# Three small tiles are padded, so that feature tiles and weight tiles start at the same place within 64 bytes

## The chip, the core and the metric

The kernel runs on one core of a Trainium2 chip. The metric is the device time of one execution in microseconds (us). Engines are named as in the profile: PE is TensorE (PEld its weight loads), DVE is VectorE, ACT is ScalarE, POOL is GpSimd, SP issues the DMAs. SBUF is the on-chip memory of 128 partitions; a tile occupies the same bytes of each partition, and "place" below means the byte in a partition at which a tile starts.

## The reference, cut to what matters

Two transformer blocks run after each other on 512 grid tokens (and 256 context tokens in the first) of 1024 features: feed-forward, a parallel mixer of two recurrences, another feed-forward; then a state-space mixer beside sparse attention, and a mixture of experts. All of it is made of dense products such as

```python
def swiglu(h, w1, w2):
    g, u = jnp.split(h @ w1, 2, axis=-1)
    return (jax.nn.silu(g) * u) @ w2

proj = h_all @ w_in
lat_out = merged[:, n_ctx:] @ w_out
```

in float32.

## The kernel before, in words

Features lie transposed, with the features on the partitions and the tokens along the free axis. To multiply in float32 quality, each operand is split in two numbers of the faster type float32r: hi (the rounded value) and lo (the rest). A product is then three matmuls into one PSUM bank, and this helper issues nearly all of them:

```python
def mm3(self, out, wh, wl, xh, xl, start, stop):
    nc.tensor.matmul(out, wh, xh, start=start, stop=False)
    nc.tensor.matmul(out, wh, xl, start=False, stop=False)
    nc.tensor.matmul(out, wl, xh, start=False, stop=stop)
```

The three are lines 210, 211 and 212 of the profile. Weights are the stationary operand (128 x 128, which is 512 bytes per partition), the features the moving one (256 or 512 columns, 1024 or 2048 bytes). In rows of the profile `pppa<-lath,whi` reads: into PSUM bank pppa, moving tile lath, stationary tile whi. Weights come by DMA into `wraw`; `wsplit` (lines 191 and 192) makes `whi` on ACT and `wlo` on DVE. Feature tiles are `lath`/`latl` (grid tokens, normed) and `ctxh`/`ctxl` (context tokens), `hh`/`hl` (hidden features of a feed-forward), `y0h`/`y0l` and `y1h`/`y1l` (the two halves of the state-space output), `mh`/`mlo` (the merged branches). Two places swap the roles: `proj_tok` (lines 552 to 554) streams the weights past stationary features, and the experts' gather (2084, 2085) streams a one-hot `oh` past `n2h`/`n2l`. The experts' own products (2109, 2132) are plain float32 and run two by two on half of the array's columns.

The stages, in us from the span's start: modulation, norms and the first feed-forward 0 to 640 (768 tokens: products of 512 and of 256 columns), the first mixer 640 to 1200, the second feed-forward 1200 to 1560 (512 tokens), norms and the start of the second block 1560 to 1690, state-space and attention 1690 to 2400, the output projections 2400 to 2520, routing 2520 to 2590, experts to the end. A scheduler sets the order of the instructions on each engine; that order is the same in both programs.

What differs is where tiles lie. Pools on the left of SBUF (constants, features) are laid one after the other from the constants on, and a tile takes a whole number of 32 bytes. Pools on the right (`wraw`, `whi`, `wlo`, temporaries) are counted from the top and don't move. Three tiles decide whether what comes after them starts at 0 or at 32 within 64 bytes: `eps` (the norms' epsilon, in the constants, ahead of everything on the left), `inv` (rotary frequencies, ahead of the second feed-forward's hidden tiles) and `frs` (the last norm's scale, ahead of `y1h`, the experts' weights `ew`, `oh`).

The starts of the main operands in the two programs, in bytes, with the place within 64 and within 256 bytes:

```
tile                          before   in 64  in 256   after    in 64  in 256
whi (first of its buffers)    186336   32     224      186336   32     224
lath                          21504    0      0        21536    32     32
ctxh                          54272    0      0        54304    32     32
hh of the first feed-forward  125120   0      192      125152   32     224
hh of the second              123104   32     224      123168   32     32
y0h                           58368    0      0        58400    32     32
y1h                           123360   32     224      123424   32     32
mh                            21504    0      0        21536    32     32
oh (moving)                   197088   32     224      197152   32     32
n2h (stationary)              74752    0      0        74784    32     32
yhl (moving)                  91136    0      0        91168    32     32
ohT (stationary)              207456   32     96       207520   32     160
ew (moving, plain float32)    123360   32     224      123424   32     32
xg (stationary)               58368    0      0        58400    32     32
hT (stationary)               a place of 32 within 64 in both
```

Buffers of one name lie a multiple of 256 bytes apart, and so do the blocks that a matmul takes out of them, so that one row speaks for all.

The program's float32r matmuls of 512 and 256 columns, and the experts' plain ones, by the places of moving and stationary operand within 64 bytes (a few odd ones left out):

```
columns   moving, stationary   before -> after      matmuls in the program
512       0, 32                -> 32, 32            5488 (lath, hh of the first feed-forward, y0, mh, yhl)
512       32, 32               -> 32, 32             648 (hh of the second feed-forward, y1)
256       0, 32                -> 32, 32            2664 (ctx, lath, mh, hh of the first feed-forward)
256       32, 0                -> 32, 32            1280 (proj_tok, the experts' gather)
256       32, 32               -> 32, 32             144 (hh of the second feed-forward, at its end)
512 plain 32, 0                -> 32, 32             256 (ew, xg)
512 plain 32, 32               -> 32, 32             128 (ew, hT)
```

By stage, the matmuls of the first sort are 1464 in the first feed-forward, 626 in the first mixer, 982 in the second feed-forward, 262 up to 1690 us, 1529 in state-space and attention, 303 in the output projections, the rest later.

Of the kernel before, what the change touches and what calls it, by code (L numbers as in the profile page):

```python
# [10 lines left out]
F32 = mybir.dt.float32  # L11
# [19 lines left out]
L = 512  # L31
# [9 lines left out]
class Kern:  # L41
# [6 lines left out]
    def banks(self, stage):  # L48
        """the eight banks of PSUM, by use, from here on"""
        pa, pb, pf = PS[stage]  # L50
        assert pa + pb + pf == 8
        if PS[max(stage - 1, 0)] == PS[stage] and stage:
            return
        self.psx.close()
        self.ps = self.psx.enter_context(self.tc.tile_pool(name="ps", bufs=1, space=PSUM, reuse_waits="tile"))
        self.psb = {"pa": pa, "pb": pb, "pf": pf}
# [13 lines left out]
    @contextmanager  # L70
    def later(self, n):
        """what is issued here yields to the next n instructions"""
        p = self.tc.cur_priority
        self.tc.cur_priority = p + n
        yield
        self.tc.cur_priority -= n
# [13 lines left out]
    def tmpf(self, name="tmpf"):  # L90
        """for work that fills gaps: not in line with the rest"""
# [10 lines left out]
    def setup(self):  # L102
# [7 lines left out]
        self.eps = cst.tile([128, 1], F32, name="eps")  # L110
        nc.vector.memset(self.eps, 1e-6)
# [8 lines left out]
    def lower_bounds(self, l0, l1, vec):  # L120
        """softmax over two rows of logits, first entry (columns [128, 8])"""
# [12 lines left out]
        # log(1 - lb)  # L134
# [4 lines left out]
    def columns(self, name, items, tag="pa"):  # L139
        """items: (key, ap of n*128 contiguous values, n); gives columns [128, n] of each."""  # L140
# [4 lines left out]
        r = 0  # L145
# [14 lines left out]
    def to_T(self, dst, src, ntok):  # L160
        """src DRAM [ntok,1024] -> dst [128, 8, ntok]"""
# [36 lines left out]
    def cols(self, w, c0, n):  # L198
        """columns c0..c0+n of w [K, N] as [128, K/128, n]"""
# [3 lines left out]
    def wrows(self, w, r0, nb):  # L203
        """row blocks r0.. (128 each) of w [K, N] as [128, nb, N]"""
# [9 lines left out]
    mvp = None      # pool of the rows' own room  # L214
# [4 lines left out]
    def silu_cols(self, aps, name):  # L219
        """columns of silu(c): [128, 8, len(aps)]"""  # L220
# [30 lines left out]
    def matvec(self, dst, w, sc, n, c0, nb, bias, tag=None):  # L251
        """dst [128, nb, n] = columns c0.. (nb blocks of 128) of silu(c) @ w + bias (bias [128, nb])"""
# [31 lines left out]
    def sumsq(self, x, n, tag, w2=None):  # L284
        """sums over the features of x^2 and, if asked for, of w2 x^2 [128 (all rows the same), n] in PSUM; x [128, 8, n]"""
# [20 lines left out]
    def table(self, name):  # L306
        """the activation table that comes next, after what has been issued"""
# [12 lines left out]
    def rstd(self, p, n, dim, name="rstd", dst=None, both=False, then=None):  # L320
        """1/sqrt(p/dim + eps) from PSUM p [128, n]; both: with the table that has both functions; then: the next table"""
# [7 lines left out]
    def halves(self, x, A, B):  # L329
        """the parts of norm_split for the grid's tokens, by half"""  # L330
        return [(x[:, :, t:t + 256], 256, A, B, t) for t in (0, 256)]

    def stats(self, parts):
        """1/rms of each of parts [(x, n, ..)]"""
# [4 lines left out]
    def norm_split(self, batches, hi, lo, rs=None):  # L339
        """batches: [[(x, n, A, B, t0)]]: hi + lo[:, :, t0:t0 + n] = x * rstd * A + B"""  # L340
# [21 lines left out]
    def ffn(self, w1, w2, hi, lo, segs, ends, begin=None, fill=()):  # L362
        """segs: [(t0, n, x, gate)]: x += gate * swiglu(hi + lo); gate already holds the half.
        ends: the segments for the first and last products, smaller for what waits and comes next"""
# [113 lines left out]
FB = (1, 1, 2)     # matrix-vector products beside a head of the mLSTM, of the HGRN, beside its last head  # L478
# [8 lines left out]
class Mix1:  # L487
    """HGRN2 and mLSTM over the context (256 tokens) and the grid (512 tokens)."""

    def mix1(self, i, hi, lo, vec, mrg, early):  # L490
        """hi, lo: [128, 8, 768] (grid tokens 0..511, context 512..767); mrg: DRAM [8, 128, 512]"""
# [36 lines left out]
    # one 128-column block, feature-major: fn(psum [128, n], t0, n)  # L528
# [11 lines left out]
    # token-major, 256 columns: fn(psum [128, 256], chunk)  # L540
# [16 lines left out]
    def wtok(self, w, c0):  # L557
        """256 columns of w, as two halves over k"""
# [10 lines left out]
    # ---------------------------------------------------------------- mLSTM  # L569
    def ml_project(self, i, w, vec):  # L570
# [10 lines left out]
        # q (chunks 0, 1: grid only) and k (chunks 2, 3), padded for the convolutions  # L581
# [3 lines left out]
        for ch in (2, 3, 0, 1):  # L585
# [15 lines left out]
            if ch == 3:  # L601
                # by half of the grid: the second one's norm comes later
# [8 lines left out]
        # v, token-major, with a column of ones  # L611
# [40 lines left out]
    def ml_scan(self, i, w, vec):  # L652
        nc, ml = self.nc, self.ml
        R = 56                                   # rows (dir, chunk, head): 0..23 forward, 32..55 backward
        # token-major gates, then rows
# [17 lines left out]
        # log sigmoid(f) = min(f, 0) - log1p(exp(-|f|))  # L673
# [8 lines left out]
        # cumulative sums and maxima within the chunks  # L682
# [6 lines left out]
        # the maximum carried from chunk to chunk  # L689
# [7 lines left out]
        ch = ml.tile([1, 4, 64], F32, name="ch")     # sum, maximum, carried m, carry weight  # L697
# [14 lines left out]
        mm = ml.tile([128, 2], F32, name="mmc")[:R]  # carried m, last maximum  # L712
# [5 lines left out]
        cwp = ml.tile([128, 2, 16], F32, name="cwp")  # [dir, (chunk, pair)]  # L718
# [17 lines left out]
        # states  # L736
# [13 lines left out]
        for c in (4, 5, 0, 1, 2, 3):  # L750
# [13 lines left out]
            if c == 5:  # L764
                # context states -> first grid chunk of each direction
# [17 lines left out]
        # queries scaled for the states  # L783
# [11 lines left out]
        # scores, outputs  # L795
# [70 lines left out]
    # ---------------------------------------------------------------- HGRN2  # L866
# [8 lines left out]
    def hg_front(self, i, w, vec, h):  # L875
        """the projections of a head and what follows from them alone"""
# [12 lines left out]
        # of each direction: the sums of the log decays, B, and A = B + log k (backward) or B - log k (forward)  # L889
# [3 lines left out]
        for d in range(2):  # L893
# [32 lines left out]
            # the keys themselves, both directions added  # L926
# [9 lines left out]
    def hg_back(self, vec, h, mrg, front):  # L936
# [3 lines left out]
        # pairs at every level  # L940
# [6 lines left out]
        for d in range(2):  # L947
            B, A, Tt = BA[:, 1 + d, :L], BA[:, 3 * d, :L], Ta[:, d, :8]
            X, Y = BA[:, 2 * d, :L], BA[:, 2 * d + 1, :L]   # what the first and the second halves take
            sq, sk = (1, 0) if d == 0 else (0, 1)      # which half holds the queries / the keys  # L950
# [46 lines left out]
            # states between the chunks  # L997
# [3 lines left out]
            # U: from the chunk's start, V: to its end; queries and keys or keys and queries  # L1001
# [20 lines left out]
            # context  # L1022
# [15 lines left out]
            # transposed keys  # L1038
# [24 lines left out]
        # scores of both directions in one [key, query] tile  # L1063
# [19 lines left out]
        # norm over the head, gate  # L1083
# [11 lines left out]
        else:  # L1095
            # nothing reads the grid's rows any more
# [22 lines left out]
class Mix2:  # L1119
    LAT = [(0, 512)]  # L1120

    # ------------------------------------------------------------- rope tables
    def rope_tables(self, i, pool, cosd, sind):
        """cos and sin of the positions' angles, [128, 512], to DRAM"""
        nc = self.nc
        inv = pool.tile([128, 1], F32, name="inv")
# [24 lines left out]
        # sin(r) = sign(r) sin(min(|r|, pi - |r|)), cos(r) = sin(pi/2 - |r|)  # L1151
# [14 lines left out]
    # ------------------------------------------------------------- projections  # L1166
    def proj_col(self, w, c0, n, fn, tag="pa"):
        """n columns from c0, feature-major over the 512 tokens: fn(psum [n, 512])"""
# [8 lines left out]
    def proj_halves(self, w, items):  # L1177
        """proj_col of up to three items (c0, n), first for one half of the tokens, then for the other: their PSUMs"""
# [1363 lines left out]
```

## Time and profile before

| what | value |
|---|---|
| runs of the kernel before | 2944.2, 2953.55, 2950.13 us; median 2950.13 |
| span of the profiled execution (first to last instruction) | 2933.2 us; no other time of that execution is on record |
| PE busy | 2799.7 us, 95% of the span |
| PE weight loads | 2114.3 us, 72%, beside the matmuls |
| DVE, ACT, POOL busy | 53%, 34%, 9% |
| DMA | 373.95 MB, mean 127 GB/s |

Busy time of PE counts overlapped matmuls once; the pace of a run of matmuls is read from their starts in the timeline, since the end of one lies behind the start of the next.

### The profile page before, as it was taken

How to read it: one execution, taken by the hardware profiler on the slowest of the kernel's cores; microseconds unless marked ns; L12 is line 12 of the kernel's file. 1: busy time of each engine (PE TensorE's matmuls, PEld its weight loads, DVE VectorE, ACT ScalarE, POOL GpSimd, SP SyncE). 2: the span in 40 equal slices, each digit the busy share in tenths (PEclk: the TensorE clock that was granted, in tenths of full speed). 3: DMA queues.
4: the chain of work that ended last, by engine and by line, in shares of the span. 5: the costliest groups of instructions: out<-in, count | busy, mean ns of one | idle time of the engine just before them, and what ended most of it. 6: DMA issues, size and time to landing. Idle time of an engine off the chain costs nothing. (4 is left out here: it accounts for less than half of the span.)

```text
span 2933.2 us, 41489 instructions
## 1 busy us (share of the span) xinstructions
PE 2799.7 (95%) x16545; PEld 2114.3 (72%) x16546; DVE 1548.8 (53%) x3002; ACT 1000.1 (34%) x1793; POOL 257.3 (9%) x301
## 2 busy tenths in 40 slices
PE   7999999999998889999998999999999999989997
PEld 5788888889786666688887777666777768855553
DVE  6333333357358995543436556655666654543334
ACT  5211112144236663322224334444444533311112
POOL 2000000002001211000001000111222120000000
PEclk9999999999999899999999999999999999999999
DMA  7422122142512348533334332101233466378885
GB/s 259 139 87 79 51 65 65 59 129 72 151 52 65 85 155 284 170 94 98 95 90 142 95 92 74 30 12 45 80 101 104 131 204 203 110 272 280 289 305 186
DMA packets 386997, 373.95 MB, mean 127 GB/s; under 512 B 20321, under 2 KB 316645, under 8 KB 386546
## 3 DMA queue, kind: packets, MB, share of 16 engines
q1 hardware_dynamic: 386802, 371.28, 40.3%
q8 instruction: 131, 2.15, 0.3%
q14 instruction: 64, 0.52, 0.1%
HBM read 343.70 MB, written 27.53 MB: 127 GB/s over the span
## 5 line engine op out<-in xcount | busy, mean ns | idle before, releaser
L191 ACT CAST whi<-wraw 128x1024 fp32r<-128x1024 f32 x277 | 285.8, 1042 | 758.9 <-PE pppa L211 340.0
L210 PE MATMUL pppa<-lath,whi 128*128 128x512 f32 (+4 forms) x1344 | 521.9, 389 | 15.0 <-ACT whi L191 6.0
L211 PE MATMUL pppa<-latl,whi 128*128 128x512 f32 (+3 forms) x1344 | 519.9, 387 | 4.7 <-DVE latl L358 3.5
L212 PE MATMUL pppa<-lath,wlo 128*128 128x512 f32 (+3 forms) x1344 | 515.2, 385 | 0.5 <-DVE wlo L192 0.5
L192 DVE TENSOR_TENSOR wlo<-wraw,whi 128x1024 fp32r<-128x1024 f32 (+1 forms) x273 | 330.8, 1218 | 255.0 <-ACT whi L191 245.5
L210 PEld LDWEIGHTS pppa<-lath,whi 128*128 128x128 f32 (+3 forms) x1344 | 252.5, 188 | 81.1 <-ACT whi L191 12.9
L211 PEld LDWEIGHTS pppa<-latl,whi 128*128 128x128 f32 (+2 forms) x1344 | 252.2, 188 | 67.6 <-DVE latl L358 5.0
L212 PEld LDWEIGHTS pppa<-lath,wlo 128*128 128x128 f32 (+2 forms) x1344 | 252.1, 188 | 58.3 <-issue 4.5
L211 PE MATMUL pppb<-hl,whi 128*128 128x512 f32 (+1 forms) x576 | 195.4, 341 | 0.0
L210 PE MATMUL pppb<-hh,whi 128*128 128x512 f32 (+1 forms) x576 | 193.1, 344 | 0.0
L212 PE MATMUL pppb<-hh,wlo 128*128 128x512 f32 (+1 forms) x576 | 191.6, 341 | 0.0
L416 DVE SCALAR_TENSOR_TENSOR xT<-pppb,sG,xT 128x512 f32<-128x512 f32 (+1 forms) x144 | 96.8, 690 | 135.0 <-PE pppb L212 134.8
L396 DVE TENSOR_TENSOR hf<-sg,pppa 128x256 f32<-128x256 f32 (+1 forms) x68 | 39.7, 584 | 232.5 <-PE pppa L212 232.0
L210 PE MATMUL pppf<-lath,whi 128*128 128x512 f32 x320 | 129.7, 405 | 7.9 <-ACT lath L1823 2.9
L2109 PE MATMUL pppa<-ew,xg 128*64 128x512 f32 x512 | 131.2, 597 | 0.0
L210 PE MATMUL pppa<-ctxh,whi 128*128 128x256 f32 (+1 forms) x440 | 124.1, 282 | 5.4 <-DVE W L912 5.1
L212 PE MATMUL pppf<-lath,wlo 128*128 128x512 f32 x320 | 127.8, 400 | 0.6 <-DVE wlo L192 0.6
L211 PE MATMUL pppf<-latl,whi 128*128 128x512 f32 x320 | 128.0, 400 | 0.0
L210 PEld LDWEIGHTS pppb<-hh,whi 128*128 128x128 f32 x576 | 108.0, 188 | 27.3 <-issue 5.8
L212 PE MATMUL pppa<-ctxh,wlo 128*128 128x256 f32 (+1 forms) x440 | 124.2, 282 | 0.0
L211 PE MATMUL pppa<-ctxl,whi 128*128 128x256 f32 (+1 forms) x440 | 123.8, 281 | 0.3 <-POOL ctxl L356 0.3
L211 PEld LDWEIGHTS pppb<-hl,whi 128*128 128x128 f32 x576 | 108.4, 188 | 16.1 <-issue 3.4
(698 smaller groups left out, 5195.5 us busy)
## 6 DMA issues: line engine op xcount, KB each, us to landing
wraw<-in_ffn_w_dram SPq DMA_DIRECT2D x132, 512.0 KB, 4.0
wraw<-in_w_in_dram SPq DMA_DIRECT2D x102, 512.0 KB, 4.2
ew<-in_w_exp_gate_dram SPq DMA_DIRECT2D x64, 512.0 KB, 9.6
ew<-in_w_exp_up_dram SPq DMA_DIRECT2D x64, 512.0 KB, 8.7
ew<-in_w_exp_down_dram SPq DMA_DIRECT2D x32, 1024.0 KB, 11.2
mraw<-in_w_mod_dram SPq DMA_DIRECT2D x40, 512.0 KB, 7.0
wraw<-in_w_mod_dram SPq DMA_DIRECT2D x32, 512.0 KB, 4.3
mraw<-in_w_ada_dram SPq DMA_DIRECT2D x32, 512.0 KB, 7.0
```

The source lines that it names most:

```text
L191: nc.scalar.copy(hi[:, :n], raw[:, :n])
L192: (nc.gpsimd if pool else nc.vector).tensor_sub(lo[:, :n], raw[:, :n], hi[:, :n].bitcast(F32))
L210: nc.tensor.matmul(out, wh, xh, start=start, stop=False)
L211: nc.tensor.matmul(out, wh, xl, start=False, stop=False)
L212: nc.tensor.matmul(out, wl, xh, start=False, stop=stop)
L396: nc.vector.tensor_mul(h[:, :n], sg[:, :n], pp[1])
L416: nc.vector.scalar_tensor_tensor(x[:, o, :], p[:, :n], gate[:, o:o + 1], x[:, o, :], op0=OP.mult, op1=OP.add)
L2109: nc.tensor.matmul(ph[x * 64:x * 64 + 64, :], xg[:, k, pr * 128 + x * 64:pr * 128 + x * 64 + 64], wts[k // 4 * 2 + x][:, k % 4, :], start= ...
```

## The change

Three tiles get 16 columns of float32 (64 bytes) where they had one or four (4 or 16 bytes, in room of 32). Only the first one or four columns are used, apart from the memset of `eps`, which fills all 16.

```diff
-        self.eps = cst.tile([128, 1], F32, name="eps")
-        nc.vector.memset(self.eps, 1e-6)
+        eps = cst.tile([128, 16], F32, name="eps")
+        nc.vector.memset(eps, 1e-6)
+        self.eps = eps[:, :1]
...
-        inv = pool.tile([128, 1], F32, name="inv")
+        inv = pool.tile([128, 16], F32, name="inv")[:, :1]
...
-        r = mo.tile([128, 4], F32, name="frs")
+        r = mo.tile([128, 16], F32, name="frs")[:, :4]
```

The rest of the diff removes comments; lines after `setup` have numbers higher by up to two in the changed file (mm3 is 212 to 214 there).

## Rows read from the trace of the kernel before

**Rows 1.** Windows by stage: length, busy PE, PEld, DVE, ACT, POOL, PE clock, DMA share, GB/s.
```profile
0.00:640.00 640.00, 616.53 (x3552) 510.31 (x3553) 247.49 (x410) 152.93 (x245) 21.83 (x29) 0.99 0.31 99
640.00:1200.00 560.00, 513.62 (x4660) 407.93 (x4659) 388.88 (x851) 276.00 (x511) 79.36 (x92) 0.95 0.43 133
1200.00:1560.00 360.00, 358.15 (x1611) 290.62 (x1610) 157.94 (x199) 93.76 (x121) 0.41 (x4) 1.00 0.31 95
...
1690.00:2400.00 710.00, 687.40 (x3589) 495.87 (x3589) 448.50 (x950) 312.42 (x636) 135.80 (x157) 0.99 0.28 82
...
2590.00:2934.00 344.00, 326.70 (x1630) 170.96 (x1628) 129.67 (x254) 54.86 (x101) 5.91 (x4) 0.98 0.79 272
```

**Rows 2.** Waits of PE, whole span: two longest; us in total, times, longest one.
```profile
PE pppf L979 <- DVE z L974: 10.0, 4, 4.9
PE pppb L2010 <- DVE pre L2006: 6.9, 2, 6.1
```

**Rows 3.** Timeline of PE, output projections: first and last of two runs of 512-column matmuls.
```profile
2432.03 0.40 PE L210 MATMUL pppa<-y0h,whi 128*128 128x512 f32 x1
...
2440.43 0.40 PE L210 MATMUL pppa<-y0h,whi 128*128 128x512 f32 x1
...
2443.20 0.39 PE L210 MATMUL pppa<-y1h,whi 128*128 128x512 f32 x1
...
2452.72 0.39 PE L210 MATMUL pppa<-y1h,whi 128*128 128x512 f32 x1
```

**Rows 4.** The same in the second feed-forward.
```profile
1299.75 0.39 PE L211 MATMUL pppb<-hl,whi 128*128 128x512 f32 x1
...
1304.05 0.39 PE L212 MATMUL pppb<-hh,wlo 128*128 128x512 f32 x1
...
1305.79 0.40 PE L210 MATMUL pppa<-lath,whi 128*128 128x512 f32 x1
...
1314.89 0.40 PE L210 MATMUL pppa<-lath,whi 128*128 128x512 f32 x1
```

**Rows 5.** Timeline of PE: first and last of three runs of 256-column matmuls.
```profile
299.79 0.28 PE L210 MATMUL pppa<-ctxh,whi 128*128 128x256 f32 x1
...
302.24 0.28 PE L210 MATMUL pppa<-ctxh,whi 128*128 128x256 f32 x1
...
700.09 0.28 PE L552 MATMUL pppa<-whi,lath 128*128 128x256 f32 x1
...
704.71 0.28 PE L552 MATMUL pppa<-whi,lath 128*128 128x256 f32 x1
...
1547.18 0.28 PE L210 MATMUL pppb<-hh,whi 128*128 128x256 f32 x1
...
1550.42 0.28 PE L210 MATMUL pppb<-hh,whi 128*128 128x256 f32 x1
```

**Rows 6.** Groups by form, whole span: count, busy us, mean ns, idle before.
```profile
L211 PE MATMUL pppa<-latl,whi 128*128 128x512 f32 x1160 | 464.6, 401 | 0.0
...
L211 PE MATMUL pppf<-latl,whi 128*128 128x512 f32 x320 | 128.0, 400 | 0.0
L211 PE MATMUL pppa<-ctxl,whi 128*128 128x256 f32 x432 | 121.6, 281 | 0.3 <-POOL ctxl L356 0.3
...
L2147 PE MATMUL pppb<-yhl,ohT 128*128 128x512 f32 x128 | 50.8, 408 | 0.1
```

**Rows 7.** Tiles xg and hT: duration ns min/median/max of the experts' plain float32 products.
```profile
L2109 PE MATMUL pppa<-ew,xg x512: 592/592/643, 2590.2 to 2904.5; 128*64 128x512 f32 x171
...
L2132 PE MATMUL pppa<-ew,hT x256: 592/592/644, 2602.8 to 2910.5; 128*64 128x512 f32 x128
```

**Rows 8.** Groups by form, windows 0:640 (two rows) and 1200:1560 (one).
```profile
L211 PE MATMUL pppa<-latl,whi 128*128 128x512 f32 x336 | 132.7, 395 | 0.0
...
L211 PE MATMUL pppb<-hl,whi 128*128 128x512 f32 x152 | 60.0, 395 | 0.0
...
L211 PE MATMUL pppb<-hl,whi 128*128 128x512 f32 x152 | 59.3, 390 | 0.0
```

## The prediction

> **What bounds the kernel now.** I read the windows by stage first. PE is busy 616.5 of the first 640 us, 358.2 of 360 in the second feed-forward, 687.4 of 710 in state-space and attention and 326.7 of 344 among the experts, where the loss lies in the tail; only the first mixer leaves more open, 46 of 560 us [rows 1]. The granted clock is 0.95 to 1.00, so nearly all of this runs at the upper of PE's two levels, 2.4 GHz. No other engine is near: DVE is at most 69% busy in any of these stages, and of these stages the DMA share passes a half only in the last. The waits of PE agree: the two longest entries are 10.0 and 6.9 us over the whole span [rows 2]. So PE is the bound, and not its waiting but its pace: what a matmul costs in an unbroken run goes almost one to one into the span.
>
> The pace is read from starts. In the output projections two runs stand next to each other, with the same helper, the same weights' buffers, the same banks and the same shape; only the feature tile differs. From 2432.03 to 2440.43 lie 12 triples of the three lines of mm3, 36 matmuls, with y0 as the moving tile: 8.40 us / 36 = 233.3 ns. From 2443.20 to 2452.72 lie 14 triples, 42 matmuls, with y1: 9.52 / 42 = 226.7 ns [rows 3]. y0 starts at 0 within 64 bytes and its weights at 32; y1 and its weights both start at 32. The second feed-forward has the same pair in another order: hh and hl (32 with weights at 32) take 4.30 us for 19 steps, 226.3 ns; lath and latl (0 with 32) 9.10 us for 39 steps, 233.3 ns [rows 4]. So before the change, in two stages and with four tiles, the one thing that goes with the faster pace is the place that the change gives to all.
>
> At 256 columns the sign turns. Context features in the first feed-forward (0 with 32): 2.45 us for 21 steps, 116.7 ns. proj_tok (32 with 0): 4.62 us for 39, 118.5 ns. The end of the second feed-forward (32 with 32): 3.24 us for 27, 120.0 ns [rows 5]. Equal places cost 3.3 ns more there than 0 with 32.
>
> **The change part by part.** The instructions and their order stay the same on every engine; the one larger instruction is the memset of eps, 16 columns for one, at the start of DVE's work, where PE still waits for data; I cost it at nothing (without that cover it would be some ns, once). No wait and no DMA is added. What changes is pace, class by class.
>
> 512 columns, 0 with 32: the program has 5488, of which the trace shows most in its largest groups (three lines of 1160, three of 320, two of 128 and so on) [rows 6]. They should go from 233.3 to 226.7 ns: 5488 x 6.67 ns = 36.6 us. 648 more have equal places before and after: nothing, if 64 bytes are what counts.
>
> 256 columns, 0 with 32: 2664 x (120.0 - 116.7) = +8.9 us. 256 columns, 32 with 0: 1280 x (120.0 - 118.5) = +2.0 us.
>
> Plain float32 products: the experts' first (32 with 0) and second (32 with 32) have the same median, 592 ns, in the same form [rows 7]. Equal places give nothing there and I cost all plain float32 work at nothing; that covers the attention's transposes and the modulation's products too, for which no clean pair of rows exists. Bounds: a step as large as the one at 256 columns, 1.5 to 3.3 ns either way, on about 256 products of that size in the expert stage, is under 1 us.
>
> DVE, ACT, POOL and DMA also see tiles moved by 32 or 64 bytes. No pair of rows here isolates that. What hides it is their idle time: DVE stands idle over 30% of each stage [rows 1], so a few per cent on its instructions would lengthen waits only in the first mixer, where PE waits on it; a gain or a loss of 5% of its longest wait there, 10.0 us [rows 2], is half a us.
>
> Sum on PE: -36.6 + 8.9 + 2.0 = -25.7 us. Not all reaches the end. By stage the 512-column part is -9.8 us (first feed-forward), -4.2 (first mixer), -6.5 (second feed-forward), -1.7, -10.2 (state-space and attention), -2.0, and -2.1 later. In the two feed-forwards PE is all but unbroken and the gain passes whole. In the mixers some of it will turn into longer waits for DVE and ACT: there PE loses 46 and 23 us already [rows 1], 8% and 3% of the stages. I take half of the first mixer's net part and a tenth of the attention stage's as lost. The first mixer's net part is small (-4.2, and +1.5 to +3 for its 256-column products), so this costs 1 to 2 us in all. That leaves -24 us.
>
> The profiled span is 2933.2 us and the median of the runs 2950.13; the 17 us between are before and after the first and last instruction and stay. So 2933 - 24 = 2909 us of span and 2950 - 24 = **2926 us**, 0.8% less. About 0.3%, 9 us, is what a measurement of this kernel can tell from no change, since its own three runs lie 9.4 us apart.
>
> One rule of the Trainium skill speaks against any gain. The page "SBUF — State Buffer" (Specifications) gives SBUF lines of 16 bytes, with a penalty for each crossing to a new line; 0 and 32 both start a line, a run of 2048 bytes crosses the same number from either, and by that the sum would be zero and the time 2950 us. The rows of y0 and y1 disagree with it as far as the pace goes: 233.3 against 226.7 ns with nothing else different.
>
> **The rivals.** (a) *The period is longer than 64 bytes.* The fast tiles of before, y1 and the second feed-forward's hh, start not only at 32 within 64 but at 224 within 256, exactly as their weights do. After the change nearly all features start at 32 within 256 and the weights still at 224, 64 bytes apart in place, a distance of which the trace of before has no clean run. If 128 or 256 bytes is the period, that distance may cost what 0 with 32 costs now. Then the 5488 gain nothing except the 456 of the first feed-forward's hh, which come to 224 and gain 3.0 us, and the 648 lose 6.67 ns each, 4.3 us: about 2951 us, no change. For it: nothing in the fast rows separates 64 from 256. Against it: the first feed-forward's hidden tiles start 32 bytes below their weights within 256, lath 32 bytes above, and both are slow alike, a mean duration of 395 ns against 390 for the second feed-forward's [rows 8]; so the slow rows, at least, show no more than the place within 64.
>
> (b) *The same, and worse: 64 bytes apart is slower than 32.* This is the case on the other side. If 64 apart costs one more step of 6.67 ns, the 5032 (5488 less 456) lose 33.6 us and the 648 lose two steps, 8.6 us, while the first hh gains 3.0: about 2989 us. It decides from some 1.4 ns per matmul on: (9 - 1.3) us / 5680 on top of (a). For it speaks only that the distance is untried; against it that both signs of a distance of 32 cost the same, so that nothing yet grows with distance.
>
> (c) *No term of the place at all*, or one that the waits take back. Then y0 and y1 differ for another reason, and the time stays at 2950 us. Against it: the second pair of rows [rows 4], in another stage with other tiles. For waits to take back more than 15 of 24 us they would have to do so in the feed-forwards, where PE has 0.5% of idle time.
>
> (d) *The 256-column cost does not come*, since it was read from a short run at the end of a stage. Then the sum is -36.6 and the time 2914 us.
>
> **How the numbers follow.** The forecast 0.67, (d) 0.06, (a) 0.11, (c) 0.07, (b) 0.09, of which a third so mild that it stays within 0.3%. Faster by over 0.3%: 0.73. Within: 0.11 + 0.07 + 0.03 = 0.21. Slower: 0.06. The forecast's own range, from 5.5 to 7 ns per matmul and 2 to 4 ns per short one, and 3 us for runs, is 2917 to 2935. The range for 8 in 10 takes (d) in below, 2914, and (a) and (c) above, to 2952; what is left out is (b) and the edges.
>
> **What would show it.** In the profile after, runs of y0 and of lath should step at 226 to 227 ns as y1 does now; a run of context features at 120 ns. The first feed-forward should lose about 4 us net (-9.8, and +5.9 for its 256-column products), the second 6.5, state-space and attention about 9, the experts under 1. If the period is longer, the new trace shows it by itself: the first feed-forward's hh would be fast and the second's hh and y1, fast now, would be slow. The prediction is wrong if the run of y1 slows or that of lath stays at 233 ns; and it is right in mechanism and wrong in size if the paces come as said and the stages don't shorten.

## The result and the profile after

The changed kernel takes 2929.17 us (median of 14 runs, 2915.01 to 2943.54), the kernel before 2946.57 us (14 runs, 2936.67 to 2955.16). The ratio is 0.994, with a 95% interval of 0.9924 to 0.9957: faster, by 17.7 us (12.7 to 22.4). The forecast was 2926 us and 24 us less. The profiled execution after took 2923.58 us with a span of 2921.8 us; the span before was 2933.2 us.

The paces are read first, at the same instructions of the program as before: these rows of the timeline of PE after the change answer to [rows 3 to 5], pair for pair (start in us, length, engine, line, tiles).

```profile
298.60 0.28 PE L212 MATMUL pppa<-ctxh,whi 128*128 128x256 f32 x1
...
300.98 0.28 PE L212 MATMUL pppa<-ctxh,whi 128*128 128x256 f32 x1
...
695.38 0.28 PE L554 MATMUL pppa<-whi,lath 128*128 128x256 f32 x1
...
699.80 0.28 PE L554 MATMUL pppa<-whi,lath 128*128 128x256 f32 x1
...
1283.77 0.39 PE L213 MATMUL pppb<-hl,whi 128*128 128x512 f32 x1
...
1288.11 0.39 PE L214 MATMUL pppb<-hh,wlo 128*128 128x512 f32 x1
...
1289.84 0.39 PE L212 MATMUL pppa<-lath,whi 128*128 128x512 f32 x1
...
1298.77 0.39 PE L212 MATMUL pppa<-lath,whi 128*128 128x512 f32 x1
...
1528.50 0.28 PE L212 MATMUL pppb<-hh,whi 128*128 128x256 f32 x1
...
1531.68 0.28 PE L212 MATMUL pppb<-hh,whi 128*128 128x256 f32 x1
...
2420.57 0.39 PE L212 MATMUL pppa<-y0h,whi 128*128 128x512 f32 x1
...
2428.80 0.39 PE L212 MATMUL pppa<-y0h,whi 128*128 128x512 f32 x1
...
2431.55 0.39 PE L212 MATMUL pppa<-y1h,whi 128*128 128x512 f32 x1
...
2441.16 0.39 PE L212 MATMUL pppa<-y1h,whi 128*128 128x512 f32 x1
```

Divided by the same numbers of steps as in the prediction:

| run | steps | before, ns | forecast | after, ns |
|---|---|---|---|---|
| lath, 512 columns | 39 | 233.3 | 226.7 | 8.93 us / 39 = 229.0 |
| y0, 512 | 36 | 233.3 | 226.7 | 8.23 / 36 = 228.6 |
| y1, 512 | 42 | 226.7 | 226.7 | 9.61 / 42 = 228.8 |
| hh of the second feed-forward, 512 | 19 | 226.3 | 226.3 | 4.34 / 19 = 228.4 |
| ctx, 256 | 21 | 116.7 | 120.0 | 2.38 / 21 = 113.3 |
| proj_tok, 256 | 39 | 118.5 | 120.0 | 4.42 / 39 = 113.3 |
| hh at the end of the second feed-forward, 256 | 27 | 120.0 | 120.0 | 3.18 / 27 = 117.8 |

The lath and y0 matmuls, 233.3 ns apart before, gained only 4.3 to 4.7 ns, and y1 and the second hh, which were to stay, lost 2.1. At 256 columns all three fell, where a rise or no change was forecast. The gain also stands in the groups by form, whose row answers to [rows 6] (401 ns before):

```profile
L213 PE MATMUL pppa<-latl,whi 128*128 128x512 f32 x1160 | 460.3, 397 | 0.0
```

The experts' plain products stay as they were, 592 ns as in [rows 7] (view of tile xg: min/median/max):

```profile
L2111 PE MATMUL pppa<-ew,xg x512: 592/592/644, 2578.4 to 2892.9; 128*64 128x512 f32 x171
```

The same pairs of rows mark off stretches of equal work in the two profiled executions:

| from | to | before, us | after, us | difference |
|---|---|---|---|---|
| start | ctx, 302.24 before | 302.24 | 300.98 | -1.3 |
| ctx | proj_tok, 704.71 | 402.47 | 398.82 | -3.7 |
| proj_tok | hl, 1299.75 | 595.04 | 583.97 | -11.1 |
| hl | hh, 1550.42 | 250.67 | 247.91 | -2.8 |
| hh | y0, 2432.03 | 881.61 | 888.89 | +7.3 |
| y0 | y1, 2452.72 | 20.69 | 20.59 | -0.1 |
| y1 | end | 480.48 | 480.64 | +0.2 |

Two stretches don't fit paces. The windows of the kernel before (columns as in [rows 1]) show two episodes of a lower clock in the third stretch:

```profile
768.00:778.00 10.00, 9.25 (x44) 2.84 (x46) 2.72 (x10) 1.82 (x8) 0.00 (x0) 0.66 0.86 279
...
800.00:812.00 12.00, 11.72 (x62) 10.33 (x61) 7.18 (x18) 1.64 (x3) 0.00 (x0) 0.72 0.37 97
```

and those of the kernel after in the fifth:

```profile
1840.00:1850.00 10.00, 10.00 (x49) 5.62 (x45) 6.36 (x17) 6.18 (x16) 1.72 (x2) 1.00 0.00 1
1850.00:1870.00 20.00, 19.82 (x94) 15.05 (x96) 8.50 (x26) 5.41 (x19) 2.90 (x4) 0.50 0.00 1
...
1905.00:1930.00 25.00, 25.00 (x108) 16.56 (x108) 11.12 (x32) 8.42 (x25) 3.16 (x5) 0.66 0.00 0
```

The granted clock fell to 0.50 at 1850 us, half of the upper level, which is 1.2 GHz, after 10 us in which PE was busy without a gap at 1.00. Counting the missing share of the clock as lost time, which is an estimate, the two episodes before cost 10 x 0.34 + 12 x 0.28 = 6.8 us, and the two after 20 x 0.50 + 25 x 0.34 = 18.5 us. Neither kernel has the other's: the other trace has 1.00 in each of these four windows. More such episodes stand elsewhere in both traces. So these two stretches tell of the clock in that execution as much as of the change.

The clock also orders the runs. Before, a run with a mean granted clock of 0.981 took 2927.42 us and one with 0.968 took 2959.44; after, 0.979 goes with 2916.09 and 0.968 with 2943.54. A straight line through the 88 runs with a clock on record (before, after, and e2 to e5 below; one more run of the kernel before, beside e8, is left out), with one slope for all and one level for each kernel, has a slope of -2160 us per 1.00 (21.6 us per 0.01) and leaves 2.2 us of scatter. At a clock of 0.973 it gives 2947.9 us before (33 runs) and 2928.5 after (22 runs): 19.4 us less. The mean clocks of the two kernels are alike, 0.9735 and 0.9729, so the change does not work through the clock.

The waits answer to [rows 2] (PE for which tile, us in total, times, longest). The first row is from the kernel before, the others from the one after; the last has the busy times after.

```profile
PE pppa L210 <- ACT whi L191: 6.0, 11, 1.1
...
PE pppf L981 <- DVE z L976: 11.9, 4, 5.0
PE pppa L212 <- ACT whi L193: 8.2, 13, 1.2
...
PE 2789.4 (95%) x16545; PEld 2119.3 (73%) x16546; DVE 1549.2 (53%) x3002; ACT 999.8 (34%) x1793; POOL 256.3 (9%) x301
```

### The profile page after: what moved, and what is told of

Its sections match the earlier page's. It is cut to its first block, busy times and chain, and to the rows that moved or that the text cites. A ratio compares the mean times of both kernels' runs of the same rounds, so it can differ in the third digit from the quotient of the medians.

```text
span 2921.8 us, 41489 instructions
## 1 busy us (share of the span) xinstructions
PE 2789.4 (95%) x16545; PEld 2119.3 (73%) x16546; DVE 1549.2 (53%) x3002; ACT 999.8 (34%) x1793; POOL 256.3 (9%) x301
## 5 line engine op out<-in xcount | busy, mean ns | idle before, releaser
L398 DVE TENSOR_TENSOR hf<-sg,pppa 128x256 f32<-128x256 f32 (+1 forms) x68 | 39.6, 583 | 226.3 <-PE pppa L214 225.8
```

Of the source, the lines that this page charges most:

```text
L398: nc.vector.tensor_mul(h[:, :n], sg[:, :n], pp[1])
```

## The experiments

The paces after the change contradict the place within 64 bytes, on which the prediction rests (theory A in the expectations). The main rival, its case (a), is a longer period (theory B). From here d is the place of the stationary operand minus that of the moving one, taken within 256 bytes. Before, lath, y0 and ctx have d = 224, hh of the first feed-forward and proj_tok 32, y1 and hh of the second 0. After, lath, y0, y1, ctx and the second hh have 192, the first hh 0, proj_tok 64.

**e1: places alone.** Runs of 48 float32r matmuls with a weight load each, all places by hand:

```python
def run(name, n, a, s):
    p = ps.tile([128, 512], F32, name=name, tag="p", bufs=8)
    for j in range(48):
        k = j % 8
        nc.tensor.matmul(p[:, :n], wt[:, k * 128 + s // 4:k * 128 + s // 4 + 128],
                         mov[:, k * 512 + a // 4:k * 512 + a // 4 + n], start=(j == 0), stop=(j == 47))
```

> This kernel leaves out the whole computation: it only times runs of 48 float32r matmuls from one moving and one stationary tile, whose distance in place is set from 0 to 480 bytes in steps of 32 (and 4, 8, 16 bytes), at 512 and at 256 columns. Theory A (64 bytes is the period, as the change has it; that lath steps at 229 ns after the change and not at 226.7 comes from other engines' accesses): all multiples of 64 alike, 226 to 227 ns at 512 columns and 120 at 256; all odd multiples of 32 alike, 233 and 117. Theory B (the period is 128 or 256): 0 and 64 differ even here, with nothing else running; 512 columns 226.7 at 0, near 229 at 64 and 192, 233 at 32 and 224; 256 columns 120 at 0, 115 at 64 and 192, 117 at 32 and 224; whether 128 equals 0 tells 128 from 256. Theory C (only the moving tile's own place counts): the pairs with both tiles moved by the same amount differ from the pair at 0.

Its timeline, 512 columns (start, length of the 48 together). The letter behind fm is s in steps of 32 bytes with a = 0: a 0, b 32, c 64, e 128, g 192, i 256. In fs both operands move by the letter, in fz the moving one alone.

```profile
25.76 11.05 PE L37 MATMUL fma<-mov,wt 128*128 128x512 f32 x48
36.65 11.35 PE L37 MATMUL fmb<-mov,wt 128*128 128x512 f32 x48
47.84 11.36 PE L37 MATMUL fmc<-mov,wt 128*128 128x512 f32 x48
...
70.28 11.32 PE L37 MATMUL fme<-mov,wt 128*128 128x512 f32 x48
...
92.64 11.16 PE L37 MATMUL fmg<-mov,wt 128*128 128x512 f32 x48
...
114.83 11.05 PE L37 MATMUL fmi<-mov,wt 128*128 128x512 f32 x48
...
328.32 11.05 PE L37 MATMUL fsc<-mov,wt 128*128 128x512 f32 x48
339.21 11.15 PE L37 MATMUL fzc<-mov,wt 128*128 128x512 f32 x48
```

From the start of one run to the next, over 48: d = 0, 32, 64, ... 224 gives 226.9, 233.1, 233.3, 234.2, 232.5, 233.3, 229.2 and 233.1 ns, and the eight from 256 on repeat them within 0.2 ns (fmi as fma). Both operands moved together by 32, 64, 128 and 256 bytes, the pace is near that of 0: 228.1, 226.9, 227.1 and 226.9. The first of these, which follows a run of 256 columns, begins slower and steps at 226.7 ns at its end. The moving one alone by 64 is d = 192, and 229.0 ns (fzc). So only the difference counts, its period is 256 bytes, and it has a sign: 192 is good, 64 is as bad as 32. Offsets of 4, 8 and 16 bytes cost too: 232.3, 230.6 and 233.3. Theories A and C fall. Of theory B the longer period holds; that 64 would be as good as 192 does not (233.3 where 229 was expected), nor do its 115 ns for 256 columns at 64 and 192 (117.9 and 117.7). The sixteen runs of 256 columns with the moving tile at 0 step at 117.3 to 119.8 ns, slowest at 0 and 160; but one with the moving tile at 64 and the stationary one at 0, also d = 192, stepped at 113.3, which e8 takes up.

fma and fmb differ by 0.30 us per 48 though as many bytes are read. The rule that the prediction quotes, the Trainium skill's lines of 16 bytes ("SBUF — State Buffer", Specifications), does not tell the two apart, since 0 and 32 both start a line, and the trace disagrees with a time of 2950 us by that rule. Nor does the Trainium skill's "TensorE: Matmul & The Clock Gate" (Part 2, step-by-step) have room for it: it gives PE two independent read ports, so that a weight load takes no read bandwidth from the running matmul, and by that their relative place would be free. The rows, 226.9 against 233.1 ns, show that it is not; they don't show why.

**e2: eps alone.** Of the three pads only the first, so that lath, ctx, y0 and the first hh lie as after, and the second hh and y1 have d = 224.

```diff
-        inv = pool.tile([128, 16], F32, name="inv")[:, :1]
+        inv = pool.tile([128, 1], F32, name="inv")
...
-        r = mo.tile([128, 16], F32, name="frs")[:, :4]
+        r = mo.tile([128, 4], F32, name="frs")
```

> The first of the three paddings alone: lath, ctx, y0, mh and the first feed-forward's hh lie as after the change, the second feed-forward's hh and y1 go to 32 bytes from their weights, the one-hot of the experts' gather too. Theory A and B both: lath keeps the pace it has after the change (229 ns), hh of the second feed-forward and y1 fall to 233 ns. Against the changed kernel 648 matmuls lose 4 ns, 2.9 us, less than a measurement tells; against the kernel before the gain stays at 14 to 16 us, ratio 0.995. If the other two paddings carried a good part of the gain, the ratio would be 0.998 or more.

2933.75 us (10 runs) against 2946.8 (14), ratio 0.996 (0.9943 to 0.9977). In its timeline y1 takes 22.16 us for 95 steps, 233.3 ns:

```profile
2439.16 0.39 PE L212 MATMUL pppa<-y1h,whi 128*128 128x512 f32 x1
...
2461.32 0.40 PE L214 MATMUL pppa<-y1h,wlo 128*128 128x512 f32 x1
```

So y1, whose place within 64 is then 32 bytes from its weights', is slow as said. By the line through the runs eps alone is worth 14.8 of the 19.4 us.

**e3: place 0 within 256.** After, with more padding, so that lath, mh, ctx, y0, y1 and the second hh have d = 0.

```diff
-        eps = cst.tile([128, 16], F32, name="eps")
+        eps = cst.tile([128, 64], F32, name="eps")
```

> The change with 64 columns for eps instead of 16: nearly all feature tiles start at the same place as their weights within 256 bytes, not only within 64 (the first feed-forward's hidden tiles at 192). Theory A: the same paces as after the change, the same time. Theory B: lath, y0 and mh step at 226.7 ns instead of 229.2, 5000 x 2.5 = 12 us less; ctx, the other 256-column products and proj_tok at 120 ns instead of 115, 2670 x 4.9 = 13 us more: about the changed kernel's time, ratio 0.994 to before, but with the two parts visible in the stages (second feed-forward shorter by 2 to 3 us, first one longer).

2923.43 us (5 runs), ratio 0.9931 (0.9903 to 0.996). Its timeline: lath 18.13 us for 80 steps, 226.6 ns; ctx 5.63 for 47, 119.8.

```profile
295.82 0.28 PE L212 MATMUL pppa<-ctxh,whi 128*128 128x256 f32 x1
...
301.45 0.28 PE L214 MATMUL pppa<-ctxh,wlo 128*128 128x256 f32 x1
...
1311.80 0.39 PE L212 MATMUL pppa<-lath,whi 128*128 128x512 f32 x1
...
1329.93 0.39 PE L214 MATMUL pppa<-lath,wlo 128*128 128x512 f32 x1
```

These are the paces that the prediction gave to the change, both at 512 and at 256 columns. They belong to d = 0. The first hh lies at 160 within 256 bytes here and so at d = 64, not at 192 as the expectation has it; at 512 columns it steps at 232.8 ns.

**e4: the same place within 64, but d = 64.** The cut between A and B in the kernel itself: the features have the place within 64 that the change gives them, but lie 64 bytes before their weights' place instead of 64 behind.

```diff
-        eps = cst.tile([128, 16], F32, name="eps")
+        eps = cst.tile([128, 48], F32, name="eps")
```

> The change with 48 columns for eps: feature tiles start at 160 within 256 bytes and weights at 224, so that both still start at 32 within 64 bytes, but the weights lie 64 bytes above the features; after the change they lie 64 below (192 above, counted round 256). Theory A (the place within 64 bytes is what counts): paces and time of the changed kernel, ratio 0.994. Theory B (the distance within 256 counts, with a sign, as the run that only times matmuls showed: 233.4 ns at 64, 229.0 at 192): lath, y0, mh, the second feed-forward's hh and y1 at 233.4 ns, no gain at 512 columns and 648 x 6 ns = 4 us lost; 256-column products near 117.8: ratio 1.000 to 1.002.

2946.27 us (12 runs) against 2945.65 (19), ratio 0.9998 (0.9977 to 1.0018): no change. Its timeline: lath 15.87 us for 68 steps, 233.4 ns; y1 18.20 for 78, 233.3; ctx 5.33 for 47, 113.4, where 117.8 was expected.

```profile
1313.98 0.40 PE L212 MATMUL pppa<-lath,whi 128*128 128x512 f32 x1
...
1329.85 0.40 PE L214 MATMUL pppa<-lath,wlo 128*128 128x512 f32 x1
```

So the same place within 64 bytes is by itself worth nothing; that the change came out at 192 and not at 64 is what it gains by. Rival (a) gave 2951 us for just this case.

**e5: each class at its best.** d = 0 for what is mostly 512 columns (lath, y0, y1, mh, the second hh), 192 for ctx, the first hh, oh and yhl.

```diff
-        eps = cst.tile([128, 16], F32, name="eps")
+        eps = cst.tile([128, 64], F32, name="eps")
...
-        inv = pool.tile([128, 16], F32, name="inv")[:, :1]
+        inv = pool.tile([128, 64], F32, name="inv")[:, :1]
...
+        b1.tile([128, 16], F32, name="padc")
...
+                self.act.tile([128, 16], F32, name="pada")
...
+            eb.tile([128, 16], F32, name="pado")
```

> Places chosen by use: lath, y0, y1, mh and the second feed-forward's hh at the same place as their weights within 256 (512 columns at 226.7 ns), ctx, the first feed-forward's hh, the experts' one-hot and yhl 64 bytes above theirs (256 columns at 115, 512 at 229). Theory A: ratio 0.994, as after the change. Theory B: against the kernel before, 4764 x 6.5 = 31 us, first hh 4, ctx 2, yhl and one-hot 2.5 us less, lath at 256 columns and proj_tok 2 us more: 37 us less on PE, some 33 us at the end, ratio 0.988 to 0.990.

2921.56 us (6 runs), ratio 0.9909 (0.9876 to 0.9941), a little less gain than expected. The least time of all kernels here, but its interval overlaps that of the change; by the line through the runs it stands at 2922.5 us, 25.3 less than before, where the change has 19.4. Its timeline has lath at 15.18 us for 67 steps, 226.6 ns, and ctx at 5.54 for 47, 117.9 where 115 was expected.

**e6: the change again,** beside the same runs of the kernel before as e4 and e5.

> The changed kernel itself beside the two above, on the same chip: ratio 0.994 as measured.

2926.67 us (8 runs) against 2945.65, ratio 0.9932 (0.9906 to 0.9957). The timeline of its profiled execution has ctx, at the instructions of the first two rows of this part, at 2.47 us for 21 steps, 117.6 ns, where the other execution of the same program had 113.3:

```profile
299.30 0.28 PE L212 MATMUL pppa<-ctxh,whi 128*128 128x256 f32 x1
...
301.77 0.28 PE L212 MATMUL pppa<-ctxh,whi 128*128 128x256 f32 x1
```

One long stretch compares all these kernels without the clock: from hl to hh in the second feed-forward the granted clock is 1.00 in every trace. These are its windows in e3 and in e4 (columns as in [rows 1]):

```profile
1295.29:1541.32 246.03, 245.55 (x1119) 203.40 (x1117) 104.28 (x125) 65.44 (x83) 0.00 (x0) 1.00 0.31 95
...
1297.11:1549.18 252.07, 251.87 (x1118) 203.43 (x1117) 104.28 (x125) 65.51 (x83) 0.00 (x0) 1.00 0.31 93
```

It took 250.67 us before, 247.91 and 247.78 after the change (second value: e6), 249.02 with eps alone (e2), 246.03 in e3, 246.09 in e5, and 252.07 in e4, where lath is as slow as before and hh slower. That is the order of the paces of lath, d = 0 first, then 192, then 64. e3 is 1.9 us shorter than the change in these 250 of the stage's 360 us, where its expectation has 2 to 3 for the whole.

**e7: columns.** The same runs as in e1 at d = 0, 32, 64 and 192 with 128 to 512 moving columns, and 64 or 32 stationary ones. Two ideas of the mechanism stood against each other: a collision of 32 cycles with the weight load (D), and a fixed cost for each distance (E).

```diff
-    def run(name, n, a, s):
+    def run(name, n, d, m=128):
...
-            nc.tensor.matmul(p[:, :n], wt[:, k * 128 + s // 4:k * 128 + s // 4 + 128],
+            nc.tensor.matmul(p[:m, :n], wt[:, k * 128 + d // 4:k * 128 + d // 4 + m],
```

> This kernel leaves out the whole computation: it only times runs of 48 matmuls at four distances of the stationary tile's place from the moving one's (0, 32, 64, 192 bytes), with 128, 256, 384 and 512 moving columns, and at 512 with 64 and 32 stationary columns. Theory D (the two streams are read beside each other; at equal place a weight load holds the moving stream up by a fixed 32 cycles of 2.4 GHz, elsewhere the moving stream runs about 9% slow throughout): at distance 0 66.7, 120, 173.3, 226.7 ns, at 32 58, 117, 175, 233 ns, so that the sign turns between 256 and 384 columns; with 32 stationary columns a quarter of the load: 217 ns at distance 0. Theory E (a fixed cost per matmul at each distance): the difference of the paces at distance 0 and 32 is the same 6.6 ns at 384 and 512 columns and with 64 and 32 stationary columns.

Its timeline (nc 384 columns, nd 512, me and mf 512 with 64 and 32 stationary columns; a is d = 0, b is 32):

```profile
37.26 8.51 PE L37 MATMUL nca<-mov,wt 128*128 128x384 f32 x48
45.61 11.08 PE L37 MATMUL nda<-mov,wt 128*128 128x512 f32 x48
56.53 11.20 PE L37 MATMUL mea<-mov,wt 128*64 128x512 f32 x48
67.56 11.28 PE L37 MATMUL mfa<-mov,wt 128*32 128x512 f32 x48
...
89.72 8.50 PE L37 MATMUL ncb<-mov,wt 128*128 128x384 f32 x48
98.06 11.36 PE L37 MATMUL ndb<-mov,wt 128*128 128x512 f32 x48
109.26 11.28 PE L37 MATMUL meb<-mov,wt 128*64 128x512 f32 x48
120.38 11.64 PE L37 MATMUL mfb<-mov,wt 128*32 128x512 f32 x48
```

From start to start: 512 columns 227.5 and 233.3 ns; 384 columns 174.0 and 173.8, and 173.3 to 174.0 over all four places, so no effect of this size; 256 columns 121.0, 119.4, 114.8 and 118.8 at d = 0, 32, 64 and 192; 128 columns 110.4 to 110.6 at every d. With 64 stationary columns 512 take 229.8 and 231.7, a step of only 1.9 ns, and with 32 they take 231.9 and 239.0, a step of 7. So a weight tile a quarter as wide makes the matmul not faster but slower at d = 0 and 32 (and at 192, 231.0 against 229.0); at 64 it is 1.4 ns faster, 231.9 against 233.3. D falls with the 231.9 ns where it has 217, E with 384 columns and with 64 stationary ones, and the mechanism stays open.

**e8: short matmuls.** 256 columns at d = 64 and 192, from different starts, each six ways in four rounds.

```diff
+    for q in range(4):
+        run("ha" + S[q], 256, 0, 64)
+        run("hb" + S[q], 256, 0, 192)
...
+        run("hd" + S[q], 256, 192, 0)
```

> This kernel leaves out the whole computation: it only times runs of 48 matmuls of 256 columns at places 64 bytes apart, in six ways (moving and stationary place 0 and 64, 0 and 192, 64 and 0, 192 and 0, 128 and 192, 192 and 128), each four times in turn, and of 512 columns at a distance of 64 and 192 from two starting places. Theory F (place alone decides, with the distance's sign): each of the six gives one pace in all its four runs, and those of equal distance agree. Theory G (at 256 columns there are two modes, near 113.5 and near 117.7 ns, and what a run starts from picks one): one and the same way shows either mode from run to run. At 512 columns both expect 233.4 at 64 and 229.0 at 192 from either start.

Its timeline (ha d = 64, hd d = 64 from another start; third letter the round):

```profile
24.50 5.82 PE L37 MATMUL haa<-mov,wt 128*128 128x256 f32 x48
...
41.46 5.61 PE L37 MATMUL hda<-mov,wt 128*128 128x256 f32 x48
...
58.22 5.60 PE L37 MATMUL hab<-mov,wt 128*128 128x256 f32 x48
...
74.55 5.82 PE L37 MATMUL hdb<-mov,wt 128*128 128x256 f32 x48
```

The same instructions on the same bytes take 117.9 ns in one round and 113.3 in the next (hd 113.5 and then 117.7), both at d = 64 and at 192, in all six ways. So at these distances 256 columns have two modes (theory G), and something other than the place picks one. It is not chance within this run: the mode changes at the same three of the six hand-overs from one run to the next (hc to hd, hd to he, hf to ha) in each round, and at none of the other three, so that it hangs on what ran before. How is not shown. The two modes fit ctx at 113.4 in e4, at 113.3 and 117.6 in the two executions of the change, and at 117.9 in e5. At 512 columns nothing of the sort shows: 233.1 ns at d = 64 and 229.2 at 192, and the same from another start.

## Why the prediction was right, and where it was not

The sign, the likeliest case (faster by over 0.3%) and nearly the time came out. But the forecast ratio, 2926 / 2950.13 = 0.9919, lies just outside the measured interval, and the sum is right in its total more than in its terms: two errors of some 15 us nearly cancel, which is luck. The mechanism, equal places within 64 bytes, is wrong by the prediction's own test, "if the run of y1 slows": it slowed from 226.7 to 228.8 ns. The paces of each class, as the mean from start to start over all neighbours of a class in the two traces, without the steps that a wait or the lower clock lengthens, and the class's number of matmuls:

| class | matmuls | before, ns | after, ns | product, us | forecast, us |
|---|---|---|---|---|---|
| lath, 512 | 4440 | 233.25 | 229.2 | -18.0 | -29.6 |
| first hh, y0, mh, yhl, 512 | 1048 | 233.1 to 234.3 | 229 to 232.4 | -3.0 | -7.0 |
| y1, second hh, 512 | 648 | 227.1 to 227.6 | 228.9 | +1.0 | 0 |
| ctx, lath, mh, both hh, 256 | 2808 | 116.7 to 119.7 | 114.5 to 119.1 | -2.4 | +8.9 |
| proj_tok, 256 | 768 | 118.3 | 115.1 | -2.5 | +1.2 |
| the experts' gather, 256 | 512 | 118.1 | 119.3 | +0.6 | +0.8 |
| sum | | | | -24.3 | -25.7 |

- **The bound.** Right. The paces sum to about -24 us and the kernel gains 17.7 (19.4 at equal clock); the idle time of PE did not grow (see the waits below). Of the rows, one is misread: 0.5% of idle time holds for the second feed-forward alone; the first has 23.5 of 640 us, 3.7% [rows 1].
- **512 columns, "They should go from 233.3 to 226.7 ns: 5488 x 6.67 ns = 36.6 us."** This is the step that failed, as a size: the term is -21, not -36.6. lath came to 229.0, which is d = 192 in e1; 226.7 belongs to d = 0, as e3 shows. The rows were read rightly; but y1 and the second hh differed from the rest in two things at once, equal places within 64 and equal places within 256 bytes, and the second was the cause. One class shows a further limit: the first hh came to d = 0 and still only to 230.8 ns. Its runs of nine stand between matmuls of 256 columns; in the rows below (timeline of PE after) the first five steps take 1.16 us, 232 ns each, and the next three 0.68, 227. So 226.7 is the pace of a run that has settled.

```profile
329.21 0.40 PE L212 MATMUL pppb<-hh,whi 128*128 128x512 f32 x1
...
330.37 0.39 PE L214 MATMUL pppb<-hh,wlo 128*128 128x512 f32 x1
...
331.05 0.39 PE L214 MATMUL pppb<-hh,wlo 128*128 128x512 f32 x1
```

- **"648 more have equal places before and after: nothing, if 64 bytes are what counts."** They are not: y1 and the second hh lost 1.3 to 1.9 ns, 1.0 us. The prediction named this as the mark of a longer period.
- **256 columns, +8.9 and +2.0 us.** Wrong in sign: about -4 us together. 120.0 ns was the pace of d = 0 (e3 has it for ctx, 119.8), not of equal places within 64. At d = 64 and 192 there are two modes, both below 120; the classes that did come to d = 0, the first hh and the gather, rose by 0.6 and 1.2 ns. That error of 15 us nearly balances the one of 16 at 512 columns.
- **The waits.** Forecast: 1 to 2 us lost in the mixers. PE's wait for whi went from 6.0 us to 8.2, and that for z from 10.0 [rows 2] to 11.9, but others fell: PE was not busy for 2933.2 - 2799.7 = 133.5 us before and for 2921.8 - 2789.4 = 132.4 after. So these traces show no loss to waits. The gap between 24 and 19.4 is not settled. The 24 comes from one execution of each kernel, and by the slope of the line, 21.6 us per 0.01 of clock, these two lie 11.4 + 13.0 = 24.4 us apart at equal clock, an estimate that agrees with their paces; the 19.4 is the mean over 55 runs.
- **Plain float32 and the memset.** The experts' plain products cost nothing, as forecast: 592 ns before and after. No row isolates the memset; e4, with one of 48 columns, stands at 0.9998.
- **By stage.** The second feed-forward was to lose 6.5 us; the stretch from hl to hh, 250 of its 360 us, lost 2.8, by an estimate 4 for the whole: the pace of lath fell by 4.3 ns instead of 6.67, and that of hh rose. The start to proj_tok lost 5.0, where the first feed-forward was to lose 4: close, by two wrong terms. For attention the two spans can't be compared as they stand, since the clock fell there for longer in one of them.
- **"the 17 us between are before and after the first and last instruction and stay"** is wrong. The time outside the span is 2923.58 - 2921.8 = 1.8 us. The profiled execution before had simply had a high clock, 0.980. The sum did not suffer, since its difference was put against the median.
- **Rival (a)** was right about the period, and e4 is the kernel that it describes. Its forecast of no change failed on a fact that no row of before held: that against d = 0, 64 bytes to one side cost 6.7 ns (e4) and to the other 2.3. The first hh, which it had at 3.0 us less, gained 1.1. What was set against it, that distances of 32 to either side are slow alike [rows 8], is true (e1: 233.1 and 233.1) but says nothing about 64. **Rival (b)** found no support: no distance that is a multiple of 32 is more than 1.1 ns slower than 32 (e1). **(c)** falls, with e4 at 0.9998 and e3 at 0.9931 and only places changed between them. **(d)** had its condition come true, but not for its reason: the cost at 256 columns did not come, since most of these pairs have places 64 bytes apart within 256. Its time of 2914 us did not come, because the term at 512 columns was too large.

## What to carry to other kernels

Where PE is the bound and each float32r matmul loads its weights, compare the paces of matmuls of one shape whose operands lie at different places, from start to start: some 4 ns of 233 per matmul were 0.6% of this kernel, and three small pads moved them. Before a step is put down to a place within some period, list the places within longer ones too: here every row at 226.7 ns agreed within 64 and within 256, and only a run with 64 but not 256 could tell them apart. Compare spans of two single executions only after the granted clock of each stretch.

## What was not expected of the hardware

- The pace of float32r matmuls of 512 columns depends on the difference of the places of stationary and moving operand, with a period of 256 bytes and a sign: 226.9 ns at 0, 229.2 at 192, 232.5 to 234.2 at the other multiples of 32 (e1). At 384 and at 128 columns it does not show (e7). After matmuls of another width a run can take some steps to reach its pace (e1, and the first hh after the change).
- 256 columns at differences of 64 or 192 run at some 113.4 or 117.8 ns, and the same instructions change between the two from round to round, always at the same hand-overs (e8), or from execution to execution (e6).
- With 32 stationary columns instead of 128, a matmul of 512 moving columns was slower at three of four distances, 231.9 instead of 227.5 ns at d = 0, and the effect of the place differs: 7 ns between 0 and 32 with 32 stationary columns, 1.9 with 64 (e7).
- Nearly all of the spread between runs of one kernel goes with the granted clock: 21.6 us per 0.01, with means from 0.967 to 0.981, and 2.2 us of scatter about the line.
